# Moving w2's operand loads, the activation sums and their splits, and adding a fourth raw weight buffer, in a one-core transformer block

## The chip, the cores and the metric

One core of one Trainium2 chip runs the whole kernel in one launch. The metric is the device time of that core in microseconds: the median of several runs. One further execution was taken by the hardware profiler; its rows are quoted below. TensorE multiplies matrices, VectorE and ScalarE work element by element, GpSimd does so too and issues DMAs, SyncE issues DMAs.

## The reference

The input is 512 tokens of 2048 features. A mixing stage (differential attention beside a gated MLP) comes first and is not touched. What matters here follows it:

```
f = rms_norm(h, ffn_norm_g)
h = h + (silu(f @ ffn_w1) * (f @ ffn_w3)) @ ffn_w2     # 2048 -> 5632 -> 2048
h = h + (p @ pl_w_up) * sigmoid(h @ pl_w_gate)         # p has 256 features
return rms_norm(h, final_norm_g)
```

All values are float32.

## The kernel before

**Precision.** A float32 operand is written as a high part (a cast to float32r, made by ScalarE) and a low part (the rest, a subtraction on VectorE). `split` (lines 130 to 139) makes both. Each product is three matmuls: high x high, low x high, high x low. In the traces the weights' parts are called `whi` and `wlo`.

**Seven products.** The products with w1 and w3 together, w2 and w_gate are made by a scheme that computes a 2 x 2 block product with seven multiplications instead of eight. The weights' blocks come as four raw tiles of 512 KB each. Sums of blocks are made on VectorE as they are needed (`prepare`, lines 249 to 273, the subtractions in `sub`, line 240). The activations' sums are made once by `sums7` (lines 203 to 207): four additions or subtractions of 128 x 256 elements for each pair of feature tiles.

**The stream.** The function `stream` (lines 209 to 341) runs a list of phases as one sequence of steps: `up1` (2 plain steps for w_up), `up_proj` (w1 and w3, 11 groups), `down` (w2, 6 groups), `up2` (2 plain steps) and `gate` (2 groups). A group has 7 products i = 0 to 6 for each of its chunks of K; with 4 chunks that is 28 steps, with 3 chunks 21. `Phase` (lines 53 to 74) gives their order: i=0 leads and i=1 follows one chunk behind (steps 0 to 7), then i=2 and 3 (steps 8 to 15), 4 and 5 (16 to 23), and 6 (24 to 27). One step is 12 matmuls of 512 columns. In iteration `now` the code first prepares the weights of step `now + 2`, then emits the matmuls of step `now`, then the jobs that a table `at` or a call of `later` has put on this step. Tiles named `raw` hold a raw weight block (i=0, 2 and 5 load one; the one of i=2 is used again by i=3 of the same chunk); tiles with the tag `b12` hold the block loaded at i=0 until i=4. `whi` and `wlo` have three buffers each.

**The scheduler.** What is written is not the final order. Each instruction goes to its engine's queue in an order that a list scheduler makes at build time: among those whose operands are ready in its simulated time, the one written first is taken. On the chip each queue then runs strictly in order. `issue_after`, used by `behind`, holds an instruction behind another one. DMAs issued by `nc.sync` stand in SyncE's queue, those by `nc.gpsimd` in GpSimd's.

**Activations of the down projection.** After each group of `up_proj`, `swiglu` (lines 371 to 416) makes 512 features of silu(a) * b. `turn` transposes them on TensorE and copies them to a tile `t8`; `spread` (lines 391 to 399) makes the sums on GpSimd and four splits of at most two sums each, in a row, into tiles named `o7` (two buffers taken in turn: one in the pool `sp`, one with the tag `c21`), and stores each to the DRAM tensor `gs`. It runs 5 and 8 steps after the group's last step. The tag `c21` also holds the result of a group's last product.

**The down projection** takes its K in three parts of 4, 4 and 3 chunks (`kws`), and for each part two groups, one for each half of the columns; both use the same operand tiles `sop`. The job `load_s` (lines 939 to 943) brings them back from `gs` in the even group: `prepare_step` calls it, by `pre`, four steps (`LEAD`) ahead of the step prepared, so the text of the program has each pair of loads six steps before the step that uses it. `done2` adds each product to the residual `h`, which `load_h` brings from DRAM; `open_ev2` (step 12) closes the pool `sp` and loads four more tiles of `h` named `d`.

**Operands of gate.** In the last group of `down` (its first step is 133, `n5`) and in `up2`, finished parts of `h` are transposed by `turn_h`, summed by `sum_h` (on GpSimd for j = 0, 1, 2, 3, 6 and 4, on VectorE for 7 and 5) and split by `split_h` into the operand tiles. The transposes go to a tile `tg` (one buffer of its own) and one of `b12`, or to `c11` and `c21`.

**The start.** In `up1` the last squares for the norm are added up by GpSimd, `rms.token` sums them over the partitions with 8 small matmuls (line 441), and `late` makes the last operands. `swap` closes the pools of the stage before.

Of the kernel before, what the change touches and what calls it, by code (L numbers as in the profile page):

```python
# [19 lines left out]
P = 128  # L20
# [17 lines left out]
LEAD = 4  # L38
# [14 lines left out]
class Phase:  # L53
# [6 lines left out]
    def __init__(self, w=None, groups=(), op=None, done=None, late=False, pre=None, plain=None,  # L60
# [3 lines left out]
        self.pre, self.plain, self.at = pre, plain, at or {}  # L64
# [13 lines left out]
def block_kernel(ctx: ExitStack, tc: tile.TileContext, out, xT, pT, w_in, w_vg, w_out, w13, w2,  # L78
# [124 lines left out]
    def sums7(at, eng):  # L203

        for o, x, y, f in ((1, 7, 6, ALU.add), (4, 0, 7, ALU.subtract), (2, 1, 0, ALU.subtract),
                           (3, 5, 2, ALU.subtract)):
            eng.tensor_tensor(at(o), at(x), at(y), op=f)  # L207

    def stream(rp, hp, bp, tp, pp, phases, nraw=3, nhalf=3, kmax=KP // 2):
# [161 lines left out]
    def swiglu(ev, sp, r, gs):  # L371
# [511 lines left out]
    def evac_u(f0, tile):  # L883
        def evac(f, s, ps):
            o = tile(s)
# [22 lines left out]
    def jobs(*items):  # L908
        d = {}
        for n, fn, *a in items:  # L910
# [3 lines left out]
    up1 = Phase(plain=(pop, w_up[0:2], evac_u(0, lambda s: b7.tile(  # L914
        [P, 2, T], F32, name="up", tag="b12", bufs=KP // 2))), at=jobs(
            (0, last_squares), (0, late, sb, KP - EARLY, *kept[0]),
            (1, late, sb, KP - EARLY, *kept[1]), (1, lambda: r.append(rms.token())),
            (2, late, sb, KP - EARLY, *kept[2]), (3, swap)))
# [20 lines left out]
    def load_s(g, i, c):  # L939
        if g % 2 == 0:  # L940
            k = 2 * sum(kws[:g // 2]) + 2 * c
            for e in range(2):
                nc.gpsimd.dma_start(out=sop[2 * c + e][:, i], in_=gs[k + e, :, i])  # L943
# [33 lines left out]
    def sum_h(j, eng):  # L977
        sums7(lambda n: t7g[j][n // 4][:, n % 4], eng)
# [8 lines left out]
    n5 = 133  # L987
    dve, gps = nc.vector, nc.gpsimd
    down = Phase(w2, [(m, 2 * sum(kws[:n]), kw) for n, kw in enumerate(kws) for m in range(2)],
                 lambda g, k: seven(sop[k]), done2, pre=load_s, at=jobs(  # L990
                     (1, load_h, 0, 0), (6, load_h, 0, 1), (6, load_h, 1, 1), (10, load_h, 1, 0),
                     (12, open_ev2),
                     (n5 + 1, turn_h, 0, "tg"), (n5 + 2, sum_h, 0, gps),
                     (n5 + 3, split_h, 0, 0), (n5 + 3, split_h, 0, 1),
                     (n5 + 4, turn_h, 1, "tg"), (n5 + 5, sum_h, 1, gps),
                     (n5 + 6, split_h, 1, 0), (n5 + 6, split_h, 1, 1),
                     (n5 + 8, turn_h, 2, "tg"), (n5 + 9, sum_h, 2, gps),
                     (n5 + 10, turn_h, 3, "c"), (n5 + 11, sum_h, 3, gps),
                     (n5 + 13, split_h, 2, 0), (n5 + 14, split_h, 3, 0),
# [203 lines left out]
```

## Time and profile before

| what | value |
|---|---|
| median of 3 runs | 2217.76 us (2215.76 to 2220.18) |
| the profiled execution | 2219.64 us, of which 2217.9 from the first instruction to the last |
| TensorE busy with matmuls | 2147.3 us, 97% |
| VectorE busy | 1648.1 us, 74% |
| ScalarE busy | 1023.9 us, 46% |
| GpSimd busy | 387.4 us, 17% |
| mean granted TensorE clock | 0.992 of full speed |
| DMA traffic | 350.28 MB, 158 GB/s on the mean |

A busy share is a mean over stages of different kinds. Matmuls overlap in TensorE's pipeline, so a busy engine need not be at its peak. An idle engine is named with the engine or transfer that ended its wait.

The stages in the profiled execution start at: `up1` 680.4 us, `up_proj` 696.3 (its group 1 at 777.6, its group 10 at 1491.8), `down` 1577.7 (its group 1 at 1665.7, its group 5 at 1957.9), `up2` 2030.2, `gate` 2046.9; gate's last matmul starts at 2204.5.

### The profile page before, as it was taken

The page shows a single profiled execution, that of the slowest core. Times are in us where ns is not written, and L with a number is a line of the kernel's source. Part 1 is how long each engine was busy: PE and PEld are TensorE (multiplying, and loading weights), DVE is VectorE, ACT ScalarE, POOL GpSimd, SP SyncE. Part 2 cuts the span into 40 slices and gives each one's busy share as a digit, 9 for nine tenths or more (in the row PEclk, how much of TensorE's full clock was granted, in tenths as well). Part 3 has the DMA queues.
Part 4 walks back from the last instruction along what each step waited for, and adds up shares of the span by engine and source line. Part 5 has one row for each costly group of instructions (what it writes and reads, how often), then busy time and mean ns, then how long its engine had stood idle before and what let it go on. Part 6 is the DMA issues. An engine that isn't in the chain of part 4 may idle for free. (4 is left out here: it accounts for less than half of the span.)

```text
span 2217.9 us, 25518 instructions
## 1 busy us (share of the span) xinstructions
PE 2147.3 (97%) x9514; PEld 1749.2 (79%) x9514; DVE 1648.1 (74%) x1650; ACT 1023.9 (46%) x1295; POOL 387.4 (17%) x490
## 2 busy tenths in 40 slices
PE   7999999999999999999999999999999999998997
PEld 5788777878887888888888887887777788877785
DVE  8777664455436888878878878887877777787896
ACT  6354323445334455455455445544433333345555
POOL 4000300002221022022022112205403102033000
PEclk9999999999999999999999999999999999999999
DMA  5453532224445453553454444359758648435535
GB/s 171 152 159 98 189 95 76 83 69 129 138 137 185 115 172 123 161 179 131 138 187 142 127 168 162 128 173 305 252 195 259 206 138 265 142 109 188 182 106 181
DMA packets 112349, 350.28 MB, mean 158 GB/s; under 512 B 12976, under 2 KB 14512, under 8 KB 112224
## 3 DMA queue, kind: packets, MB, share of 16 engines
q1 hardware_dynamic: 67904, 233.86, 34.0%
q0 software_dynamic: 41056, 107.16, 14.3%
q10 hardware_dynamic: 3264, 7.62, 0.9%
q8 instruction: 75, 1.23, 0.2%
q14 instruction: 50, 0.41, 0.1%
HBM read 286.46 MB, written 62.13 MB: 157 GB/s over the span
## 5 line engine op out<-in xcount | busy, mean ns | idle before, releaser
L320 PE MATMUL c<-whi,op 128*128 128x512 f32 x4592 | 1427.5, 392 | 5.8 <-ACT whi L133 4.3
L320 PEld LDWEIGHTS c<-whi,op 128*128 128x128 f32 x4592 | 862.6, 189 | 184.2 <-ACT whi L133 5.1
L320 PE MATMUL c<-wlo,op 128*128 128x512 f32 x2296 | 903.2, 393 | 25.9 <-DVE wlo L134 25.2
L133 ACT CAST whi<-raw 128x1024 fp32r<-128x1024 f32 (+1 forms) x331 | 346.5, 1049 | 485.3 <-PE c L320 286.5
L134 DVE TENSOR_TENSOR wlo<-raw,whi 128x1024 fp32r<-128x1024 f32 (+1 forms) x331 | 417.2, 1265 | 199.4 <-ACT whi L133 194.5
L320 PEld LDWEIGHTS c<-wlo,op 128*128 128x128 f32 x2296 | 433.0, 189 | 134.9 <-DVE wlo L134 44.6
L133 ACT CAST whi<-t 128x1024 fp32r<-128x1024 f32 x246 | 258.6, 1052 | 271.4 <-PE c L320 244.3
L169 PE MATMUL ps<-op,whi 128*128 128x512 f32 x1088 | 349.0, 400 | 0.0
L134 DVE TENSOR_TENSOR wlo<-t,whi 128x1024 fp32r<-128x1024 f32 x246 | 308.3, 1255 | 22.0 <-ACT whi L133 21.5
L240 DVE TENSOR_TENSOR t<-raw,t 128x1024 f32<-128x1024 f32 x164 | 208.3, 1270 | 134.7 <-DMA raw<-w 115.4
L169 PEld LDWEIGHTS ps<-op,whi 128*128 128x128 f32 x1088 | 201.3, 188 | 44.3 <-issue 3.8
L169 PE MATMUL ps<-op,wlo 128*128 128x512 f32 x544 | 213.4, 392 | 0.0
L207 POOL TENSOR_TENSOR t<-t 128x256 f32<-128x256 f32 x88 | 106.5, 1210 | 541.1 <-ACT t L388 537.5
L133 ACT CAST whi<-b 128x1024 fp32r<-128x1024 f32 x82 | 86.3, 1054 | 123.3 <-PE c L320 114.7
L943 POOL DMA_DIRECT2D op<-gs x154 | 81.7, 535 | 298.5 <-PE c L320 284.3
L240 DVE TENSOR_TENSOR t<-b,raw 128x1024 f32<-128x1024 f32 x82 | 102.4, 1249 | 27.2 <-DMA raw<-w 23.4
L169 PEld LDWEIGHTS ps<-op,wlo 128*128 128x128 f32 x544 | 102.1, 188 | 21.6
L240 DVE TENSOR_TENSOR b<-raw,b 128x1024 f32<-128x1024 f32 x82 | 106.1, 1294 | 8.4 <-DMA raw<-w 7.5
L134 DVE TENSOR_TENSOR wlo<-b,whi 128x1024 fp32r<-128x1024 f32 x82 | 100.5, 1225 | 8.5 <-ACT whi L133 8.2
L133 ACT CAST o<-t 128x512 fp32r<-128x512 f32 x88 | 49.9, 567 | 105.6 <-DMA gs<-o 54.6
L344 DVE TENSOR_TENSOR c<-c,c 128x1024 f32<-128x1024 f32 x63 | 76.8, 1219 | 11.6 <-PE c L320 11.0
L453 POOL TENSOR_TENSOR r<-v,mhalf 128x1 f32<-128x1 f32 (+1 forms) x23 | 17.3, 752 | 383.7 <-DVE v L449 383.7
(177 smaller groups left out, 1321.2 us busy)
## 6 DMA issues: line engine op xcount, KB each, us to landing
raw<-w SPq DMA_DIRECT2D x198, 512.0 KB, 3.7
op<-gs POOLq DMA_DIRECT2D x154, 256.0 KB, 4.5
b<-w SPq DMA_DIRECT2D x66, 512.0 KB, 4.6
gs<-o POOLq DMA_DIRECT2D x66, 512.0 KB, 3.6
raw<-w_in SPq DMA_DIRECT2D x40, 512.0 KB, 3.6
raw<-w_out SPq DMA_DIRECT2D x32, 512.0 KB, 3.6
raw<-w_vg SPq DMA_DIRECT2D x24, 512.0 KB, 3.8
raw<-w_gate SPq DMA_DIRECT2D x24, 512.0 KB, 3.7
```

The source lines that it names most:

```text
L133: recent[:] = (nc.scalar.copy(out=hi, in_=src), nc.vector.tensor_tensor(out=lo, in0=src, in1=hi.bitcast(F32), op=ALU.subtract))
L134: nc.vector.tensor_tensor(out=lo, in0=src, in1=hi.bitcast(F32), op=ALU.subtract))
L169: nc.tensor.matmul(ps[:, m], lhsT=a[:, j, ms], rhs=op[k][:, b], start=k == 0 and i == 0, stop=k == nk - 1 and i == 2)
L207: eng.tensor_tensor(at(o), at(x), at(y), op=f)
L240: nc.vector.tensor_tensor(o, x, y, op=ALU.subtract)
L320: product[:] = [nc.tensor.matmul(p, lhsT=f.op(g, k)(i, x, s), rhs=y[:, e], start=k == 0 and i in (0, 1, 5) and (x, y) == (0, whi), stop=k ...
L344: (eng or nc.vector).tensor_tensor(o, x, y, op=ALU.add)
L453: nc.gpsimd.tensor_tensor(r[:, :n], v[:, :n], mhalf[:, :n], op=ALU.pow)
L943: nc.gpsimd.dma_start(out=sop[2 * c + e][:, i], in_=gs[k + e, :, i])
```

## The change

1. `stream` gets four raw buffers instead of three (`nraw=4`).
2. `load_s` is no longer called by `pre` six steps ahead. `loads` places each pair of loads in the table `at`: spread evenly from the first step of the group before the even group (a group of the part before, or the last of `up_proj`) to five steps ahead of the even group's end, though never ahead of the step after the old operand's last use.
3. `spread` is cut in parts: `add7` makes the sums, on VectorE, and each of the eight splits of a group has a step of its own, 5, 6, 8, 9, 11, 14, 17 and 20 steps after the group's end. Their `o7` tiles take the tags `c21` and `c12`; `sp` keeps only `t8`.
4. `sums7` always runs on VectorE, so `sum_h` goes into `split_h`; `both_h` makes both parts. Their places are moved by a step or so.
5. The tile `tg` is replaced by one of the raw buffers.
6. `load_h` and `open_ev2` are moved to later steps (1, 6, 10, 22 and 20).
7. In `up1`'s table `rms.token` moves from step 1 to step 4 and `swap` from 3 to 5, which are steps 2 and 3 of `up_proj`.
8. The evacuations of `up2` take `c12`, `c22`, a `b12` buffer and `c12`, instead of `c12` and `c22` twice.

```
-    def stream(rp, hp, bp, tp, pp, phases, nraw=3, nhalf=3, kmax=KP // 2):
+    def stream(rp, hp, bp, tp, pp, phases, nraw=4, nhalf=3, kmax=KP // 2):
...
-            if n + LEAD < len(steps) and steps[n + LEAD][0].pre:
-                f, *a = steps[n + LEAD]
-                f.pre(*a)
...
-        def spread(j, q):
+        def add7(q):
             t = c[q]
-            sums7(lambda n: t[:, n], nc.gpsimd)
-            for n in range(0, 7, 2):
-                m = min(2, 7 - n)
-                o = (ev[0].tile([P, 2, 2, 256], F32R, name="o7", tag="c21", bufs=1) if n % 4 else
-                     sp[0].tile([P, 2, 2, 256], F32R, name="o7", bufs=1))
-                split((o[:, :m, 0], o[:, :m, 1]), t[:, n:n + m])
-                nc.gpsimd.dma_start(out=gs[j, :, n:n + m], in_=o[:, :m].bitcast(F32))
+            sums7(lambda n: t[:, n])
+
+        def spread(j, q, n, tag):
+            m = min(2, 7 - n)
+            o = ev[0].tile([P, 2, 2, 256], F32R, name="o7", tag=tag, bufs=1)
+            split((o[:, :m, 0], o[:, :m, 1]), c[q][:, n:n + m])
+            nc.gpsimd.dma_start(out=gs[j, :, n:n + m], in_=o[:, :m].bitcast(F32))
...
-                    later(5 + 3 * q, spread, 2 * g + q, 2 * q)
+                    later(5 + 2 * q, add7, 2 * q)
+                    for k, n in enumerate((11, 14, 17, 20) if q else (5, 6, 8, 9)):
+                        later(n, spread, 2 * g + q, 2 * q, 2 * k, "c21" if q or k % 2 == 0 else "c12")
...
-            (1, late, sb, KP - EARLY, *kept[1]), (1, lambda: r.append(rms.token())),
-            (2, late, sb, KP - EARLY, *kept[2]), (3, swap)))
+            (1, late, sb, KP - EARLY, *kept[1]), (2, late, sb, KP - EARLY, *kept[2]),
+            (4, lambda: r.append(rms.token())), (5, swap)))
...
+    def loads():
+        for n, kw in enumerate(kws):
+            before = up_proj if n == 0 else down
+            last = [a[2:] for a in before.steps if a[1] == (2 * n - 1 if n else HT // 4 - 1)]
+            g0 = down.first[2 * n]
+            use = [a[2:] for a in down.steps if a[1] == 2 * n]
+            for j, (i, c) in enumerate(use):
+                t = -len(last) + j * (len(last) + len(use) - 6) // (len(use) - 1)
+                yield g0 + max(t, last.index((i, c)) - len(last) + 1), 2 * sum(kws[:n]) + 2 * c, 2 * c, i
...
-        if a == "tg":
-            t = (ev2[0].tile([P, 4, 256], F32, name="tg", bufs=1),
-                 b7.tile([P, 4, 256], F32, name="tg", tag="b12", bufs=KP // 2))
+        if a == "b":
+            t = [p.tile([P, 4, 256], F32, name="tg", tag=n, bufs=4) for p, n in ((w7, "raw"), (b7, "b12"))]
...
         if n:
             split((o[:, 4:7, 0], o[:, 4:7, 1]), t[:, 0:3])
         else:
+            sums7(lambda n: t7g[j][n // 4][:, n % 4])
             split((o[:, 0:4, 0], o[:, 0:4, 1]), t)
...
+    down.at.update(jobs((1, load_h, 0, 0), (6, load_h, 1, 1), (10, load_h, 0, 1),
+                        (20, open_ev2), (22, load_h, 1, 0),
+                        (n5 + 1, turn_h, 0, "b"), (n5 + 2, both_h, 0),
+                        (n5 + 4, turn_h, 1, "b"), (n5 + 5, both_h, 1),
+                        (n5 + 8, turn_h, 2, "b"), (n5 + 10, turn_h, 3, "c"),
+                        (n5 + 13, split_h, 2, 0), (n5 + 14, split_h, 3, 0),
...
+    def evac_tile(f, s):
+        p, n = (b7, "b12") if (f, s) == (1, 0) else (ev[0], "c22" if (f, s) == (0, 1) else "c12")
...
+        (0, split_h, 6, 1), (0, both_h, 7), (0, turn_h, 4, "b"),
+        (1, turn_h, 5, "c"), (1, both_h, 4)))
...
-                     (0, split_h, 5, 0), (0, split_h, 5, 1),
+                     (0, both_h, 5),
```

## Rows read from the trace of the kernel before

**Rows 1.** Windows: length, busy time and count per engine, clock, DMA share, GB/s.

```profile
core 0: us, PE busy (x) PEld busy (x) DVE busy (x) ACT busy (x) POOL busy (x), PEclk, DMA share, GB/s
680.40:777.60 97.20, 92.96 (x401) 75.74 (x401) 77.62 (x75) 47.63 (x51) 6.89 (x5) 0.96 0.47 146
777.60:1491.80 714.20, 708.64 (x3170) 579.93 (x3169) 587.83 (x531) 360.09 (x424) 127.08 (x144) 1.00 0.47 153
1491.80:1577.70 85.90, 80.86 (x353) 65.36 (x352) 65.75 (x59) 40.02 (x48) 42.43 (x72) 0.98 0.96 305
1577.70:1665.70 88.00, 82.20 (x353) 66.24 (x352) 67.02 (x60) 36.18 (x42) 18.22 (x25) 0.96 0.58 192
1665.70:1957.90 292.20, 288.00 (x1261) 235.91 (x1260) 224.81 (x193) 110.68 (x106) 53.36 (x101) 1.00 0.66 199
1957.90:2030.20 72.30, 66.06 (x301) 52.79 (x300) 60.91 (x49) 36.22 (x50) 30.86 (x24) 0.98 0.36 118
2030.20:2204.70 174.50, 167.86 (x737) 137.72 (x736) 149.11 (x142) 94.92 (x122) 6.26 (x8) 0.99 0.49 156
```

**Rows 2.** Windows of the streaming matmuls alone (line 320): PE, PEld, clock, DMA.

```profile
1755.00:1875.00 120.00, 120.00 (x531) 99.38 (x530) 1.00 0.57 171
2008.20:2011.20 3.00, 3.00 (x7) 2.42 (x8) 0.50 0.55 175
```

**Rows 3.** Timeline of TensorE: start, length, instruction, count.

```profile
703.97 1.03 PE L828 MATMUL pt<-ident,ho 128*128 128x128 f32 x8
```

**Rows 4.** Waits of TensorE, 680.4 to 2204.5: total, times, longest.

```profile
PE c L320 <- DVE wlo L134: 25.2, 28, 4.6
...
PE pt L968 <- ACT tg L975: 3.2, 1, 3.2
PE pt L441 <- POOL acc L432: 2.9, 1, 2.9
```

**Rows 5.** Waits of ScalarE, the same stretch.

```profile
ACT o L133 <- DMA gs<-o: 54.6, 30, 4.5
ACT o L133 <- POOL t L207: 51.0, 32, 2.7
```

**Rows 6.** Waits of VectorE, the same stretch.

```profile
DVE t L240 <- DMA raw<-w: 138.8, 80, 5.7
```

**Rows 7.** Timeline of VectorE in up group 7.

```profile
1297.54 1.22 DVE L240 TENSOR_TENSOR t<-raw,t 128x1024 f32<-128x1024 f32 x1 [2.51 <-DMA raw<-w]
1298.68 1.22 DVE L134 TENSOR_TENSOR wlo<-b,whi 128x1024 fp32r<-128x1024 f32 x1
1299.81 1.22 DVE L240 TENSOR_TENSOR t<-raw,t 128x1024 f32<-128x1024 f32 x1
```

**Rows 8.** Timeline of GpSimd, up group 10 and down group 0.

```profile
1531.92 6.05 POOL L943 DMA_DIRECT2D op<-gs  x11
...
1620.53 1.56 POOL L929 DMA_DIRECT2D d<-hnat  x3
```

**Rows 9.** All loads of line 943: durations, first and last start, landing times.

```profile
L943 POOL DMA_DIRECT2D op<-gs x154: 527/527/634, 1494.3 to 1897.6; - x154
...
DMA to landing us min/median/max: 2.9/4.5/9.6
```

**Rows 10.** Groups of VectorE by form, 696.3 to 2030.2: busy, mean ns, idle before.

```profile
L134 DVE TENSOR_TENSOR wlo<-raw,whi 128x1024 fp32r<-128x1024 f32 x198 | 252.6, 1282 | 59.6 <-ACT whi L133 59.3
L134 DVE TENSOR_TENSOR wlo<-t,whi 128x1024 fp32r<-128x1024 f32 x198 | 250.0, 1264 | 16.1 <-ACT whi L133 15.9
L240 DVE TENSOR_TENSOR t<-raw,t 128x1024 f32<-128x1024 f32 x132 | 169.2, 1282 | 115.9 <-DMA raw<-w 115.4
L240 DVE TENSOR_TENSOR b<-raw,b 128x1024 f32<-128x1024 f32 x66 | 86.7, 1313 | 8.4 <-DMA raw<-w 7.5
```

**Rows 11.** The sums of line 207: ns min/median/max, first and last start.

```profile
L207 POOL TENSOR_TENSOR t<-t x88: 724/1182/1830, 787.4 to 1606.3; 128x256 f32<-128x256 f32 x88
...
L207 DVE TENSOR_TENSOR c<-c x4: 407/410/411, 2031.7 to 2051.3; 128x256 f32<-128x256 f32 x4
```

More of the change, by code (lines that the diff above doesn't have):

```diff
@@ L53, with __init__ @@
 class Phase:
-    def __init__(self, w=None, groups=(), op=None, done=None, late=False, pre=None, plain=None,
+    def __init__(self, w=None, groups=(), op=None, done=None, late=False, plain=None,
                  at=None, order=None):
@@ L63, in __init__ @@
         self.w, self.groups, self.op, self.done, self.late = w, groups, op, done, late
-        self.pre, self.plain, self.at = pre, plain, at or {}
+        self.plain, self.at = plain, at or {}
         self.steps = [(self, -1, f, 0) for f in range(plain[1].shape[0])] if plain else []
@@ L201, in moving7, with sums7 @@
         return o
[L203 removed]
+    def sums7(at):
         for o, x, y, f in ((1, 7, 6, ALU.add), (4, 0, 7, ALU.subtract), (2, 1, 0, ALU.subtract),
                            (3, 5, 2, ALU.subtract)):
[L207 to L209 removed]
+            nc.vector.tensor_tensor(at(o), at(x), at(y), op=f)
+    def stream(rp, hp, bp, tp, pp, phases, nraw=4, nhalf=3, kmax=KP // 2):
         steps = [s for f in phases for s in f.steps]
@@ L884, in evac @@
         def evac(f, s, ps):
-            o = tile(s)
+            o = tile(f, s)
             with tc.high_priority(PRIO):
@@ L937, in open_ev2, with load_s @@
                 load_h(u, f)
[L939 to L943, printed above, removed]
+    def load_s(k, p, i):
+        for e in range(2):
+            nc.gpsimd.dma_start(out=sop[p + e][:, i], in_=gs[k + e, :, i])
+    def loads():
[7 more added lines that the diff above has]
+                yield g0 + max(t, last.index((i, c)) - len(last) + 1), 2 * sum(kws[:n]) + 2 * c, 2 * c, i
     def done2(g, i, acc, later, s=slice(None)):
@@ L984, in split_h, with both_h @@
         else:
+            sums7(lambda n: t7g[j][n // 4][:, n % 4])
             split((o[:, 0:4, 0], o[:, 0:4, 1]), t)
-    n5 = 133
-    dve, gps = nc.vector, nc.gpsimd
+    def both_h(j):
+        for n in range(2):
+            split_h(j, n)
     down = Phase(w2, [(m, 2 * sum(kws[:n]), kw) for n, kw in enumerate(kws) for m in range(2)],
[L990 to L999, printed above, removed]
-                     (n5 + 17, load_p),
-                     (n5 + 18, split_h, 2, 1), (n5 + 18, turn_h, 6, "tg"),
-                     (n5 + 19, split_h, 3, 1), (n5 + 19, sum_h, 6, gps), (n5 + 19, turn_h, 7, "c"),
-                     (n5 + 20, sum_h, 7, dve), (n5 + 20, split_h, 6, 0)))
@@ L1004, in block_kernel @@
-    up2 = Phase(plain=(pop, w_up[2:4], evac_u(2, lambda s: ev[0].tile(
-        [P, 2, T], F32, name=("c12", "c22")[s], bufs=1))), at=jobs(
-            (0, split_h, 6, 1), (0, split_h, 7, 0), (0, split_h, 7, 1),
-            (0, turn_h, 4, "tg"), (0, sum_h, 4, gps),
-            (1, turn_h, 5, "c"), (1, sum_h, 5, dve),
-            (1, split_h, 4, 0), (1, split_h, 4, 1)))
-    assert down.first[5] == n5
+                 lambda g, k: seven(sop[k]), done2)
+    n5 = down.first[5]
+    down.at.update(jobs((1, load_h, 0, 0), (6, load_h, 1, 1), (10, load_h, 0, 1),
[4 more added lines that the diff above has]
+                        (n5 + 13, split_h, 2, 0), (n5 + 14, split_h, 3, 0),
+                        (n5 + 17, load_p),
+                        (n5 + 18, split_h, 2, 1), (n5 + 18, turn_h, 6, "b"),
+                        (n5 + 19, split_h, 3, 1), (n5 + 19, turn_h, 7, "c"),
+                        (n5 + 20, split_h, 6, 0)))
@@ new lines, in block_kernel @@
+    for n, *a in loads():
+        f, n = (up_proj, n + len(up_proj.steps)) if n < 0 else (down, n)
+        f.at.setdefault(n, []).append((load_s, a))
+    def evac_tile(f, s):
+        p, n = (b7, "b12") if (f, s) == (1, 0) else (ev[0], "c22" if (f, s) == (0, 1) else "c12")
+        return p.tile([P, 2, T], F32, name="up", tag=n, bufs=4 if p is b7 else 1)
+    up2 = Phase(plain=(pop, w_up[2:4], evac_u(2, evac_tile)), at=jobs(
+        (0, split_h, 6, 1), (0, both_h, 7), (0, turn_h, 4, "b"),
+        (1, turn_h, 5, "c"), (1, both_h, 4)))
@@ L1017, in extra @@
     def extra(tag):
-        return {"b12": b7, "raw": w7, "tg": ev2[0], "d": ev2[0]}[tag].tile(
-            [P, 2, T], F32, name="last", tag=tag, bufs={"raw": 3, "tg": 1}.get(tag, 4))
+        return {"b12": b7, "raw": w7, "d": ev2[0]}[tag].tile([P, 2, T], F32, name="last", tag=tag, bufs=4)
     def load_last(u, f, *tags):
@@ L1118, in block_kernel @@
                      (43, load_last, 0, 3, "b12", "b12"), (46, load_last, 1, 3, "b12", "b12"),
-                     (47, load_last, 1, 2, "tg", "raw"), (49, load_gains, 2),
+                     (48, load_last, 1, 2, "raw", "raw"), (49, load_gains, 2),
                      (50, load_last, 0, 2, "raw", "raw")))
```

5 lines of the change are left out of this document (1 added, 4 removed).

## The prediction

> **What bounds the kernel now.** I read the stages first, then TensorE's waits, then what each waited-for engine was itself waiting for. The change touches nothing before 680.4 us except the size of one buffer ring, and nothing after TensorE's last gate matmul at 2204.7, so only this stretch counts. In a stretch without a wait, 529 matmuls start in 120 us (531 records touch the window, two of them only at its edges), 0.2267 us each [rows 2]; eight transposes take 1.03 us with the pipeline's tail of the last, about 0.11 each [rows 3]. A streaming step is 12 matmuls, 2.72 us. A stage's length less its matmuls and transposes at these prices is what TensorE lost there, slow clock included [rows 1]:
>
> - start (two plain steps, first up group): 97.2 - 384 x 0.2267 - 16 x 0.11 = 8.4
> - up groups 1 to 9: 714.2 - 3024 x 0.2267 - 144 x 0.11 = 12.8
> - up group 10: 85.9 - 336 x 0.2267 - 16 x 0.11 = 8.0
> - down group 0, the same work: 88.0 - 77.9 = 10.1
> - down groups 1 to 4: 292.2 - 1260 x 0.2267 = 6.6
> - down group 5: 72.3 - 252 x 0.2267 - 48 x 0.11 = 9.9
> - the two later plain steps and gate: 174.5 - 720 x 0.2267 - 16 x 0.11 = 9.5
>
> The sum, 65 us or 2.9%, is the ceiling of any gain here. The reader is to see that TensorE is the bound and that the losses are local. It waits mostly for `wlo`, VectorE's half of a weight split (25.2 us in 28 waits), once for an accumulator (2.9), once for a copy of `tg` (3.2) [rows 4]. A long wait costs twice: just after TensorE's waits around 2007, the granted clock is 0.50, the lower of its two levels (1.2 of 2.4 GHz), and seven matmuls fill 3 us [rows 2].
>
> Behind `wlo` stand two things. VectorE sits idle for a raw weight tile, 80 times, 138.8 us together, up to 5.7 [rows 6], while a released buffer refills; in [rows 7] it waits 2.51 us for one tile and only then makes the subtraction and the `wlo` that TensorE needs. And ScalarE, which casts `whi` in the same queue, stands still in the splits of the activations: 54.6 us for stores to `gs` out of the two `o7` buffers and 51.0 for GpSimd's sums [rows 5].
>
> **The fourth raw buffer.** Of a chunk's four loads three pass through `raw`: for steps i=0, 2 and 5. The i=2 tile lives until i=3. Within a group of 28 steps, with three buffers, the fourth i=2 load (used at step 13) gets the buffer freed at step 10; those for steps 18 and 20 get buffers freed at 12 and 14. With four, every chunk keeps its own buffer and the same loads are freed at 5, 10 and 12: at least 8 steps or 22 us ahead instead of 3 or 8.2 us. The slowest `op<-gs` transfer took 9.6 us to land [rows 9], and raw transfers share the same DMA engines. So I take these waits as nearly gone; bounds: none, if something else holds the queue of SP, and all.
>
> **The loads of w2's operands.** 154 DMAs before and after. Now the first leaves at 1494.3 [rows 9], just after step 0 of up group 10; its place in the program is near step 22 of that group (down step -6). So the emitted order runs such a load as soon as its slot's last reader is done, some 22 steps ahead of its place: two per step through one whole group. Group 10 thus moves 305 GB/s at a DMA share of 0.96, while the groups before it move 153 [rows 1]; when GpSimd's queue was held by `gs` stores, eleven loads left at once at 1531.92 [rows 8]. The new places lie at most 22 steps behind the same dependence. I therefore hold it more likely than not (6 in 10) that the loads still leave at once and the spreading does little. It matters only if raw loads are late, which the fourth buffer prevents; value 0, bounds 0 to the 11 us of the rival below.
>
> **Sums on VectorE.** 112 sums leave GpSimd (88 of swiglu at a median of 1.18 us, the others of the last down group and of the second plain phase). On VectorE one takes 0.41 [rows 11]: 112 x 0.41 = 46 us. Against it stands what GpSimd takes from VectorE. A full subtraction takes 1.22 us where GpSimd is idle [rows 7]; in this stretch the four groups average 1282, 1264, 1282 and 1313 ns [rows 10], an excess of 198 x 0.062 + 198 x 0.044 + 132 x 0.062 + 66 x 0.093 = 35 us, and the half-size splits add to it. So VectorE's total barely changes.
>
> The rows show a stretch of the overlapped instructions. The Trainium skill (SBUF — State Buffer, Who interferes with whom) goes further: a VectorE instruction with two SBUF inputs and a GpSimd one that reads SBUF contend for an exclusive port, and the loser blocks for the whole instruction. By that, as an estimate, VectorE could win back up to 112 x 1.18 = 132 us instead of 35, the waits left in up groups and down group 5 below would go too, and the sum would be near 2172, still inside the forecast's band; the measured averages do not show that much.
>
> What counts is the backlog at the worst place. Starts of full operations lie 1.14 us apart [rows 7]; half-size splits I put at 0.6. TensorE needs `wlo` 0.45 us into a step, and ScalarE may cast `whi` two steps earlier (three buffers), so VectorE's lead is 2 x 2.72 + 0.45 - 1.05 (cast) - 1.22 = 3.6 us. In steps 4 to 9 of a group the new order asks VectorE for 3.4, 1.7, 5.1, 4.0, 1.5 and 3.4 us (preparation of the step two ahead, 4 x 0.41 for `add7` in steps 4 and 6, splits) against 2.72 per step, 3.16 in steps 4 and 5 with their transposes. The backlog peaks at 3.6, just the lead: I leave half a microsecond per group, 5 us over groups 1 to 9. Splits every few steps also let each `gs` store land before its buffer is wanted, which takes the 54.6 us away from ScalarE's queue; the 51.0 shrink to VectorE's shorter sums.
>
> **Down group 5 and after.** The same count with `both_h` (4 x 0.41 + 1.14 + 0.88) in steps 2 and 5 peaks at 7.0, 3.4 over the lead; later splits and gate's first steps with `both_h` 4 and 5 exceed it by some 2.5. So 5 us of 9.9 stay, and 6 of 9.5 (the end of gate keeps its own). The evacuation that reused `c12`, behind the 3.2 us wait, goes to another buffer.
>
> **Start.** The accumulator's wait (2.9) and the half-clock step behind it (2.2) go when the token's matmuls come three steps later; TensorE then meets VectorE's work on the last operands earlier, so I count 4.3 of 8.4. **Down group 0.** Its loss follows a burst of `d` loads at 1620.53 [rows 8], which now leaves near step 20; with raw tiles held early I leave 2.5 of 10.1. Up group 10 keeps 1.5 of 8.0, down groups 1 to 4 keep 2 of 6.6. Moved loads of `h` change queue places, not counts; GpSimd's queue gets emptier. Should `c12` come back late for step 13, VectorE's addition would hold its queue; its cover is about 1.5 steps, and without it the cost is one such wait, some 4 us.
>
> **Sum.** 4.1 (start) + 5 + 1.5 + 2.5 + 2 + 5 + 6 = 26 us stay of 65: a gain of 39. The profiled execution took 2219.64 (span 2217.9), so 2180.4; the median of the runs, 2217.76, lies 1.9 lower, which gives 2178.5. I say 2180 because a new order of all queues seldom comes without one new wait.
>
> **Rivals.**
> - *The loads still come in a burst and starve the weights.* The demand in group 10 is some 336 GB/s, 26 MB in 78 us, near what [rows 1] show at a share of 0.96. Then group 10 and down 1 to 4 keep their losses: 2180 + 11 = 2191. Against it: 8 steps of lead. 0.11.
> - *The ring is not used*, since SP issues in order and a load of `b` waits at its head. Then up groups 1 to 10, down 1 to 4 and half of down group 0 keep theirs: 23 us of the gain go, 2203. 0.11.
> - *VectorE becomes the bound (slower).* It decides at the lead of 3.6 us: if the excess in [rows 10] is not GpSimd's doing, the sums come on top, 3.3 us per group; each up group waits that long and then runs a step at the lower clock (2.5): 11 x 5.8 = 64, down group 5 another 7, less 39: 2252. For it: the backlog count stands exactly at the lead. Against it: 1.22 without GpSimd in [rows 7]. 0.08. The Trainium skill (Perfetto Trace Analysis, Optimizing Scalar/DVE Operations) speaks for this rival: work may be offloaded from a saturated VectorE, to GpSimd even, though it adds that the shared port can spoil that; VectorE is busy 82% in [rows 1], and the change goes the other way.
> - *All waits vanish*: 2155. 0.07. *Gains and new waits cancel*: about 2217. 0.05.
> - The forecast, between 2167 and 2190: 0.58.
>
> **Range and chances.** 0.2% (4.4 us) is about what a measurement of this kernel can tell from no change. The range leaves out the slower rival, the cancelling one and most of the case where all waits vanish: 2160 to 2207. Faster: 0.58 + 0.11 + 0.11 + 0.07 = 0.87; same 0.05; slower 0.08.
>
> **What would show it.** Right: VectorE's waits for raw tiles fall from 138.8 to under 40 us; ScalarE's waits for `gs` stores are gone; full subtractions average 1.22; no accumulator wait ahead of up step 0. The loads' first start and the rate in up group 10 tell whether they spread. Wrong: waits for `wlo` in steps 6 to 10 of every group would mean that VectorE's backlog was undercounted; raw transfers landing after more than 15 us would mean that the DMA engines were.

## The result, and the profile after

2186.68 us median (2183.3 to 2187.53) against 2218.97 (2215.76 to 2221.66) for the kernel before on the same chip: a ratio of 0.9852, interval 0.9834 to 0.987. The profiled execution took 2185.85 us, its span 2183.7. The forecast was 2180, its range 2160 to 2207.

The stages of the kernel after, in windows (length, busy time and count per engine, clock, DMA share, GB/s), answer to [rows 1]:

```profile
core 0: us, PE busy (x) PEld busy (x) DVE busy (x) ACT busy (x) POOL busy (x), PEclk, DMA share, GB/s
684.10:785.90 101.80, 94.14 (x401) 75.77 (x402) 76.37 (x74) 46.25 (x51) 6.92 (x5) 0.95 0.41 129
785.90:1488.70 702.80, 702.80 (x3170) 581.63 (x3169) 581.81 (x603) 362.55 (x424) 38.70 (x72) 1.00 0.49 155
1488.70:1571.50 82.80, 78.83 (x354) 64.40 (x352) 64.56 (x67) 40.06 (x48) 34.09 (x64) 1.00 1.00 317
1571.50:1651.70 80.20, 79.14 (x354) 64.27 (x353) 66.52 (x68) 35.82 (x43) 8.90 (x17) 1.00 0.61 210
1651.70:1937.30 285.60, 285.60 (x1262) 236.49 (x1261) 225.57 (x192) 110.87 (x106) 54.55 (x101) 1.00 0.66 203
1937.30:2001.70 64.40, 63.47 (x302) 52.07 (x301) 60.02 (x68) 37.21 (x51) 2.13 (x4) 1.00 0.36 120
2001.70:2170.20 168.50, 166.18 (x737) 136.30 (x735) 148.79 (x147) 94.30 (x121) 2.25 (x3) 1.00 0.50 164
```

TensorE's loss in a stage is its length less matmuls at 0.2267 us and transposes at 0.11, as in the prediction. The same sum over windows of every later run gives this table; the first column is the start of the first plain matmul, "up", "down" and "gate" are the stages of [rows 1].

```
                      first  start up1-9  up10 down0 down1-4 down5 gate   sum
before                680.4    8.4  12.8   8.0  10.1     6.6   9.9  9.5  65.3
forecast                 -     4.1   5     1.5   2.5     2     5    6    26
after                 684.1   12.9   1.5   4.9   2.2     0.0   2.0  3.6  27
1  pT first           681.2    8.2   1.6   2.9   1.6     0.9   2.0  2.9  20
2  ring of three      680.5    7.4   5.3   9.6   1.1     8.3   2.2  4.0  38
3  old token          684.3   14.5   2.8   4.1   1.7     0.9   2.0  3.2  29
4  sums on GpSimd     683.5   14.0  11.1   7.4   6.4     1.0   2.0  3.0  45
5  after, again       683.7   14.3   1.5   5.9   2.8     1.0   2.0  3.0  31
7  splits bunched     677.9    8.0   6.6   3.6   7.1     0.3   2.0  2.1  30
8  splits early       679.2    9.1   5.8   7.7   6.1     1.0   2.0  2.8  35
9  loads held         679.2    8.2   1.5   7.3   4.9     0.2   2.0  3.4  28
10 tiles moved        679.6    9.3  14.2   6.3   1.6     6.1   2.9  5.6  46
11 squares on VectorE 679.3    7.9   1.5   4.0   0.9     0.5   2.0  3.0  20
12 no loads           678.9    9.1   2.4   0.2   0.2     2.1   2.0  2.4  18
```

(Runs 1, 7 to 12 hold pT first as well; run 6 stands with run 9.) Each row comes from one execution. Two executions of the same kernel, "after" and 5, differ by up to 1.4 us in a stage, so a difference of that size is read only where a wait in the trace accounts for it.

What the reader is to see: the gain that the forecast counted is there, and more, except in up group 10, which kept 4.9 us instead of 1.5, and at the start, which lost instead of gaining. Over the whole stretch TensorE's waits for `wlo` fall from 25.2 us to 7.1, and the one for `tg` is gone:

```profile
PE c L316 <- DVE wlo L133: 7.1, 7, 2.5
```

At the start, 684 to 786 us, TensorE's waits (total, times, longest) are these, to hold against [rows 4]:

```profile
PE c L316 <- ACT op L198: 5.7, 2, 4.9
PE c L298 <- ACT pop L132: 4.7, 1, 4.7
PE c L316 <- DVE op L199: 1.2, 1, 1.2
```

The accumulator's wait of 2.9 is gone. In its place TensorE waits 4.7 us for `pop`, the operand of the plain matmuls, made from the transfer of pT, and 4.9 and 1.2 at up step 6 for the last operand of the up half; behind each of them the granted clock is at or near its lower level, 0.58 from 684.1 to 687.5 and 0.51 from 722 to 729 (window, columns as above):

```profile
722.00:729.00 7.00, 4.18 (x9) 2.88 (x10) 6.26 (x5) 1.56 (x1) 0.00 (x0) 0.51 0.00 0
```

Why `pop` is late is on SyncE's queue. The kernel before, then after, in the timeline of its issues (start, length with its waits, transfer, count):

```profile
671.08 0.80 SPq L230 DMA_DIRECT2D raw<-w_up  x2
671.92 0.43 SPq L230 DMA_DIRECT2D raw<-w  x1
672.40 0.43 SPq L865 DMA_DIRECT2D pr<-pT  x1
```

```profile
669.95 0.80 SPq L229 DMA_DIRECT2D raw<-w_up  x2
670.80 6.63 SPq L229 DMA_DIRECT2D raw<-w  x4
677.48 0.43 SPq L863 DMA_DIRECT2D pr<-pT  x1
```

Before, the ring of three was full after three raw transfers, and pT came next. With a fourth buffer SyncE has four `raw<-w` to issue first, and waits among them for a buffer to come free; pT leaves 5.1 us later than before, lands 5.9 us after that, and the cast of `pop` starts at 683.4.

Waits of VectorE and of ScalarE, 684 to 2170, answer to [rows 6] and [rows 5]:

```profile
DVE t L239 <- DMA raw<-w: 64.7, 55, 3.1
DVE b L239 <- DMA raw<-w: 18.0, 20, 2.9
```

```profile
ACT o L132 <- DMA gs<-o: 48.1, 25, 5.8
ACT o L132 <- DVE t L206: 18.8, 11, 3.3
```

VectorE's groups by form, 700 to 2000 (busy, mean ns, idle before), answer to [rows 10], and the loads' first and last start and landing times to [rows 9]:

```profile
L133 DVE TENSOR_TENSOR wlo<-t,whi 128x1024 fp32r<-128x1024 f32 x197 | 240.2, 1220 | 27.8 <-ACT whi L132 26.2 <-PE pt L975 1.5
L133 DVE TENSOR_TENSOR wlo<-raw,whi 128x1024 fp32r<-128x1024 f32 x196 | 238.8, 1221 | 75.8 <-ACT whi L132 75.5
L239 DVE TENSOR_TENSOR t<-raw,t 128x1024 f32<-128x1024 f32 x132 | 161.3, 1222 | 65.3 <-DMA raw<-w 64.7
L239 DVE TENSOR_TENSOR b<-raw,b 128x1024 f32<-128x1024 f32 x66 | 80.6, 1221 | 18.5 <-DMA raw<-w 18.0
...
L133 DVE TENSOR_TENSOR o<-t,o 128x512 fp32r<-128x512 f32 x66 | 45.3, 686 | 5.9 <-ACT o L132 5.9
L206 DVE TENSOR_TENSOR t<-t 128x256 f32<-128x256 f32 x88 | 36.9, 419 | 0.0
```

```profile
L939 POOL DMA_DIRECT2D op<-gs x154: 540/540/554, 1491.2 to 1877.9; - x154
...
DMA to landing us min/median/max: 2.9/4.7/11.2
```

### The profile page after: what moved, and what is told of

It is laid out like the page before. It is cut to its first block, busy times and chain, and to the rows that moved or that the text cites. A ratio compares the mean times of both kernels' runs of the same rounds, so it can differ in the third digit from the quotient of the medians.

```text
span 2183.7 us, 25457 instructions
## 1 busy us (share of the span) xinstructions
PE 2130.8 (98%) x9514; PEld 1745.2 (80%) x9514; DVE 1640.0 (75%) x1762; ACT 1026.9 (47%) x1295; POOL 249.1 (11%) x378
## 5 line engine op out<-in xcount | busy, mean ns | idle before, releaser
L133 DVE TENSOR_TENSOR wlo<-raw,whi 128x1024 fp32r<-128x1024 f32 (+1 forms) x331 | 403.3, 1221 | 216.8 <-ACT whi L132 211.9
L316 PEld LDWEIGHTS c<-wlo,op 128*128 128x128 f32 x2296 | 431.3, 188 | 101.5 <-DVE wlo L133 11.2
L133 DVE TENSOR_TENSOR wlo<-t,whi 128x1024 fp32r<-128x1024 f32 x246 | 299.8, 1220 | 34.0 <-ACT whi L132 32.3
L239 DVE TENSOR_TENSOR t<-raw,t 128x1024 f32<-128x1024 f32 x164 | 200.5, 1222 | 78.4 <-DMA raw<-w 64.7
L395 POOL DMA_DIRECT2D gs<-o x88 | 47.3, 538 | 768.0 <-DVE o L133 718.1
L239 DVE TENSOR_TENSOR b<-raw,b 128x1024 f32<-128x1024 f32 x82 | 100.1, 1221 | 20.1 <-DMA raw<-w 18.0
L132 ACT CAST o<-t 128x512 fp32r<-128x512 f32 x88 | 49.1, 569 | 76.3 <-DMA gs<-o 48.1
L524 PE MATMUL c<-op,whi 128*128 128x512 f32 x192 | 61.9, 404 | 9.0 <-ACT whi L132 9.0
```

The source lines that it names most:

```text
L132: recent[:] = (nc.scalar.copy(out=hi, in_=src), nc.vector.tensor_tensor(out=lo, in0=src, in1=hi.bitcast(F32), op=ALU.subtract))
L133: nc.vector.tensor_tensor(out=lo, in0=src, in1=hi.bitcast(F32), op=ALU.subtract))
L239: nc.vector.tensor_tensor(o, x, y, op=ALU.subtract)
L316: product[:] = [nc.tensor.matmul(p, lhsT=f.op(g, k)(i, x, s), rhs=y[:, e], start=k == 0 and i in (0, 1, 5) and (x, y) == (0, whi), stop=k ...
L524: nc.tensor.matmul(ps[:, m], lhsT=a[:, n, m * P:(m + 1) * P], rhs=xop[k][:, b], start=k == 0 and i == 0, stop=k == KT - 1 and i == 2)
```

## The experiments

Ratios are to the kernel before in the same set of runs, whose median was 2213.18 us for runs 1 to 4, 2214.37 for 5 to 8, 2216.71 for 9 to 11 and 2215.51 for 12; beside the kernel after it was 2218.97, so times of different sets are compared by their ratios.

**1. pT first on SyncE's queue.**

```diff
-        nc.sync.dma_start(out=pr, in_=pT)
+        with tc.high_priority(10 * PRIO) if high else nullcontext():
+            nc.sync.dma_start(out=pr, in_=pT)
```

> The changed kernel, but the transfer of pT (1024 elements a row, the operand of the first plain matmuls) is put ahead of all raw transfers on SP's queue. Theory A (the fourth raw buffer let SP issue more raw transfers ahead of pT, and one of these waits for a slot, so pT is issued 5 us later than before and the start loses its gain): the first plain matmul moves back from 684.1 to about 680, the 4.7 us wait on the cast of pop goes, the half-clock step and the wait at up step 6 shrink with it; 2186.7 less about 8 is 2178 to 2180. Theory B (the moved rms token and swap, with the subtractions queued ahead of the last operand's sums on VectorE, make the start late): the first plain matmul comes earlier, but the wait at up step 6 grows by as much; 2185 to 2188.

2173.94 us, ratio 0.9823 (0.9807 to 0.9838), where the kernel after had 0.9852 and, in run 5, 0.9876. Timeline of SyncE's issues and TensorE's waits up to 777 us:

```profile
660.05 0.33 SPq L864 DMA_DIRECT2D pr<-pT  x1
671.89 0.80 SPq L229 DMA_DIRECT2D raw<-w_up  x2
```

```profile
PE c L316 <- DVE wlo L133: 2.9, 2, 1.8
PE c L316 <- ACT whi L132: 1.6, 1, 1.6
```

The waits for `pop` and at up step 6 are both gone: theory A. ScalarE's and VectorE's orders in this stretch shift a little with the new place, so whether step 6 was late only by the late plain steps or also by that order isn't separated. 4.5 us of other waits, at up steps 4 and 5, keep the start at a loss of 8.2.

This run also shows what the moved token is worth once pT is early. GpSimd's sum for the norm, then TensorE's first matmuls of up step 0:

```profile
693.34 4.63 POOL L430 TENSOR_TENSOR acc<-acc,sq 128x512 f32<-128x512 f32 x2 [26.43 <-ACT sq L429]
```

```profile
693.10 0.62 PE L316 MATMUL c<-whi,op 128*128 128x512 f32 x2
```

The sum ends at 697.97, 4.9 us after step 0 begins; in run 2, where pT is early too, it ends at 694.89 and step 0 begins at 691.86, 3.0 us. With the token ahead of step 0, as in the kernel before, TensorE would have had to wait some 3 to 5 us. This is an estimate from these rows: no run has tried the old token with pT early, and the old place could shift the sum as well.

**2. Three raw buffers** (small edits that fit the later users of the `raw` tiles to three buffers are left out here).

```diff
-    def stream(rp, hp, bp, tp, pp, phases, nraw=4, nhalf=3, kmax=KP // 2):
+    def stream(rp, hp, bp, tp, pp, phases, nraw=3, nhalf=3, kmax=KP // 2):
```

> The changed kernel with three raw buffers instead of four (the last load that had its fourth one gets a tile of its own). Theory A: the pT transfer is issued where it was before, so the start gets its 8 us back; but the waits for raw weights return everywhere else. The forecast priced the fourth buffer at 20 to 25 us, so 2186.7 - 8 + 23 = about 2200 (2193 to 2207), with VectorE's waits for raw weights back above 100 us. Rival (the sums that left GpSimd and the even stores took the stalls away, the fourth buffer did little): 2178 to 2184, VectorE's waits for raw weights near the changed kernel's 83 us.

2189.8 us, 0.989 (0.9873 to 0.9907). pT is issued at 672.14 and the first plain matmul starts at 680.5, without any priority: the second proof of what delayed it. Elsewhere the waits are back (VectorE, 681 to 2177):

```profile
DVE t L239 <- DMA raw<-w: 134.2, 92, 6.2
```

By the table, against run 1, up 1 to 10 and down 1 to 4 lose 23.2 instead of 5.4: the fourth buffer is worth 17.8 us. The time is 10 us under the 2200 expected: 5.8 is the chip, on which the kernel before was faster by that, and the forecast's 23 was some 5 too high. Of this 23, 3.8 stood for half of down group 0, which loses no more with three buffers (1.1) than with four (1.6).

**3. Token and swap at their old steps.**

```diff
-            (4, lambda: r.append(rms.token())), (5, swap)))
+            (1, lambda: r.append(rms.token())), (3, swap)))
```

> The changed kernel with the rms token and the swap of pools back at steps 1 and 3 of the first plain phase (from 4 and 5). Theory A (late pT): the start stays as late as it is, and the wait for the accumulator ahead of up step 0, some 4 us with its half-clock step, comes back: 2187 to 2191. Theory B (the moved token and swap cost the start): the wait at up step 6 of some 6 us goes, 2179 to 2183.

2187.55 us, 0.9888 (0.9871 to 0.9905). The waits at steps 5 and 6 stay (7.4 us for `op`, longest 4.8), the one for `pop` too, and 0.8 us for the accumulator come back. Theory B falls, and theory A is right on the late pT but not on its 4 us for the accumulator. Beside the late pT the plain steps end 5.0 us later than in the kernel before (696.8 for 691.7) and GpSimd's sum only 3.0 (697.55 for 694.55), so most of the wait is hidden: the 0.8 us is the price of the old place beside a late pT, and not beside an early one (run 1).

**4. The sums of the up half on GpSimd.**

```diff
-            sums7(lambda n: t[:, n])
+            sums7(lambda n: t[:, n], nc.gpsimd)
```

> The changed kernel with the activation sums of the up half (seven products' sums, 256 wide, four a tile) back on GpSimd; ring of four and spread splits stay. Theory A (the sums on GpSimd stretch VectorE's full operations and make the splits wait): full subtractions rise from 1.22 to about 1.28 us on average, the up groups lose 5 to 10 us again: 2190 to 2197. Rival (with the fourth buffer the stretch is covered, and VectorE is rid of 40 us of sums): 2184 to 2188.

2200.89 us, 0.9944 (0.9931 to 0.9958): slower than theory A asked for. Three groups of VectorE, 700 to 2000, its timeline beside GpSimd's sums in the eighth up group, the window of up groups 1 to 9, and ScalarE's waits:

```profile
L133 DVE TENSOR_TENSOR wlo<-t,whi 128x1024 fp32r<-128x1024 f32 x195 | 252.2, 1294 | 18.7 <-ACT whi L132 17.2 <-PE pt L975 1.5
...
L239 DVE TENSOR_TENSOR t<-raw,t 128x1024 f32<-128x1024 f32 x131 | 170.2, 1299 | 73.1 <-DMA raw<-w 71.5
...
L133 DVE TENSOR_TENSOR o<-t,o 128x512 fp32r<-128x512 f32 x66 | 56.1, 861 | 6.4 <-ACT o L132 6.3
```

```profile
1275.30 1.23 DVE L133 TENSOR_TENSOR o<-t,o 128x512 fp32r<-128x512 f32 x1
1276.45 1.75 DVE L239 TENSOR_TENSOR b<-raw,b 128x1024 f32<-128x1024 f32 x1
```

```profile
786.30:1498.80 712.50, 706.82 (x3170) 580.11 (x3169) 595.53 (x531) 361.66 (x424) 132.31 (x144) 1.00 0.47 153
```

```profile
ACT o L132 <- DMA gs<-o: 120.4, 57, 5.5
```

VectorE has 72 instructions fewer in up 1 to 9 and is busy 13.7 us longer: beside a sum, in these rows, a full operation takes 1.75 us instead of 1.22, and the half-size one that ends a split 1.23 instead of 0.69. ScalarE waits 120 us for the stores instead of 48; each store is released by such a split, but how much of the 72 us that explains wasn't taken apart. Up 1 to 10 and down 0 lose 24.9 instead of 10.2 in run 5.

**5. The kernel after once more**, without an edit.

> The changed kernel unchanged, on the chip of the three runs beside it, so that their ratios stand beside its own: 0.985 of the time before (0.983 to 0.987).

2187.62 us, 0.9876 (0.9857 to 0.9894): a little above the range expected, its interval overlapping that of the result (0.9834 to 0.987).

**6 and 9. Loads held to their steps.**

```diff
+        lo = ready[now + 1][1].bitcast(F32)[:, 0, 0:1]
+        v = sm.tile([P, 1], F32, name="held")
+        op = nc.gpsimd.tensor_tensor(v, lo, mhalf[:, 0:1], op=ALU.mult)
+        with tc.issue_after(op.ins):
             for e in range(2):
                 nc.gpsimd.dma_start(out=sop[p + e][:, i], in_=gs[k + e, :, i])
```

> The changed kernel with pT first (as in the first run) and with each pair of operand loads held to its planned step: a GpSimd operation of one column on the newest low half of the weights stands ahead of the two loads, so they can't leave before that step. Theory A (the loads leave two a step in the last up group because the queue has nothing to wait for; they slow the raw weights there): their first issue is spread over the group and the next, the raw weights land sooner, the last up group loses under 1.5 us instead of 2.9, the total is 1 to 3 us below the kernel with pT first alone (ratio 0.981 to 0.982). Theory B (the loads are hidden either way, and holding them only brings them nearer to their use): the last up group gains under 1 us and the down group after it loses as much or more; ratio 0.982 to 0.985.

2207.82 us, 0.9968 (0.9956 to 0.998), and the nine up groups, in which nothing is held, lost 14.2: an artefact, told with run 10. Run 9 writes `v` into a tile that was there:

```diff
-        v = sm.tile([P, 1], F32, name="held")
+        v = sm.tile([P, 4], F32, name="v")[:, 0:1]
```

> The held loads once more, with the GpSimd operation writing into a tile that was there already: in the run before, its own small tile moved every tile behind it by 128 bytes, and the matmuls of all up groups, nine of which have no held load in them, ran at a pitch of 230 to 240 ns instead of 227. Theory A (the moved tiles cost the pitch, the holding itself costs or gains little): the nine up groups are back at a loss under 3 us, the total is within 4 us of the kernel with pT first (ratio 0.980 to 0.984), and only now the loss of the last up group and of the first down group tells what an even return is worth (below 2.9 + 1.6 = 4.5 us: a gain). Theory B (the holding itself slows the whole, by its waits on the low halves): the time stays near the run before, ratio 0.994 to 0.998.

2180.83 us, 0.9842 (0.9829 to 0.9856), and up 1 to 9 are back at 1.5: theory A, as far as the place of the tiles goes. The windows of up 10 and down 0 show that the loads now do spread, 240 and 273 GB/s:

```profile
1479.10:1564.30 85.20, 80.83 (x353) 65.45 (x352) 64.41 (x67) 39.86 (x47) 39.14 (x57) 0.98 0.76 240
1564.30:1647.20 82.90, 79.66 (x354) 64.09 (x353) 66.70 (x68) 35.72 (x43) 29.34 (x51) 1.00 0.83 273
```

Yet both stages lose more, 7.3 and 4.9 us. GpSimd's timeline and then ScalarE's tell why:

```profile
1500.46 5.52 POOL L946 TENSOR_TENSOR v<-wlo,mhalf 128x1 f32<-128x1 f32 x1 [3.40 <-DVE wlo L133]
1505.92 1.11 POOL L949 DMA_DIRECT2D op<-gs  x2
1507.03 1.06 POOL L399 DMA_DIRECT2D gs<-o  x2
```

```profile
1513.01 0.41 ACT L132 CAST o<-t 128x256 fp32r<-128x256 f32 x1 [8.25 <-DMA gs<-o]
1513.32 1.04 ACT L132 CAST whi<-t 128x1024 fp32r<-128x1024 f32 x1
```

Two stores stand behind the holding operation, ScalarE waits 8.25 us for their buffer, and the cast that TensorE needs stands behind ScalarE's wait. So this hold costs, and the spreading itself was not yet priced; run 12 does that.

**7. The four splits of a tile at one step**, and **8. splits early**, both with two store buffers in turn:

```diff
-                    for k, n in enumerate((11, 14, 17, 20) if q else (5, 6, 8, 9)):
+                    for k, n in enumerate((8, 8, 8, 8) if q else (5, 5, 5, 5)):
```

(in run 8: 8, 9, 9, 10 and 5, 5, 6, 6)

> The changed kernel with pT first, and with the four splits of a tile at one step again (two buffers in turn), sums still on VectorE. Theory A (spreading is what keeps VectorE's backlog under its lead): sums and four splits in a row are 4 x 0.42 + 4 x 0.69, about 4.4 us of VectorE beside its regular work, twice a group; the nine up groups lose 5 to 15 us instead of 1.6, ratio 0.985 to 0.989. Rival (with the fourth raw buffer the lead covers it): groups lose 1 to 3 us as now, and ScalarE's waits for the stores, 48 us now, shrink, since two buffers take turns; ratio 0.981 to 0.983.

> The changed kernel with pT first, and the splits two at steps 5 and 6 and one to two at 8 to 10, two buffers in turn, so that all stores leave before the second half of a group. Theory A (ScalarE's waits for the one store buffer, at steps 11 to 20, hold up casts of the weights in the last up group, where loads make a store land in 6 us): ScalarE's waits for the stores fall below 25 us and the last up group loses about 1 us less than with pT first alone; the rest as there, ratio 0.981 to 0.982. Rival (a denser set of splits costs VectorE's lead): up groups lose 3 to 8 us instead of 1.6, ratio 0.983 to 0.986.

2186.46 us, 0.9874 (0.9858 to 0.989), and 2187.71, 0.9875 (0.986 to 0.989). Against run 1, up 1 to 9 lose 5.0 and 4.2 us more, and down 0 5.5 and 4.5. In run 8 up 10 also loses 4.8 more, which is not explained here. Most of the loss in down 0 is one wait of about 4 us, whose releaser the profile doesn't name. The rows ahead of it tell more; run 7's GpSimd, VectorE and TensorE:

```profile
1602.90 1.08 POOL L928 DMA_DIRECT2D d<-hnat  x2
```

```profile
1611.37 1.23 DVE L239 TENSOR_TENSOR t<-raw,t 128x1024 f32<-128x1024 f32 x1 [5.33 <-DMA raw<-w]
```

```profile
1614.97 0.70 PE L316 MATMUL c<-whi,op 128*128 128x512 f32 x2 [4.05 <-issue]
```

With the stores gone early, the loads named `d` leave 38.6 us into down 0 (53.8 in run 1), VectorE then waits 5.33 us for a raw tile, and TensorE's wait ends right behind. Run 8 has the same three: 37.8 us, 5.60 and 4.29. So the loss in down 0 looks like the old burst of `d` loads, come back because no store stands ahead of them in GpSimd's queue; no run moves these loads alone.

ScalarE's waits for the stores are 45.6 and 44.0 us where run 1 has 54.9, and its copies of an accumulator now wait for stores as well. Theory A of run 7 holds at its lower end in the up groups; in run 8 the rival does, a little slower yet than it said.

**10. All tiles moved by 128 bytes.**

```diff
+    nc.vector.memset(sm.tile([P, 1], F32, name="held"), 0.0)
```

> The kernel with pT first, and nothing else but a small tile of one column, cleared once at the start, which moves every tile allocated behind it by the same 128 bytes. Theory A (the place of the tiles sets the pitch): matmuls of the up groups at 230 ns and more on average, the nine up groups lose 10 to 15 us, ratio 0.99 to 0.996. Theory B (the place does not matter): as with pT first alone, 0.981 to 0.984.

2199.8 us, 0.9926 (0.9913 to 0.9938). Up groups 1 to 9 of run 1, then of this run:

```profile
778.20:1481.20 703.00, 703.00 (x3170) 581.62 (x3169) 581.77 (x603) 362.24 (x424) 38.62 (x72) 1.00 0.49 155
```

```profile
777.80:1493.30 715.50, 715.50 (x3169) 583.23 (x3168) 584.58 (x603) 362.42 (x424) 38.61 (x72) 1.00 0.48 152
```

TensorE is never idle in either, its clock is 1.00, and the same matmuls take 12.5 us longer. That is theory A, and it is what had spoilt run 6: less the transposes at 0.11 it is 0.2314 us a matmul instead of 0.2272. The streaming matmuls of no other run than 6 and 10 have the longer pitch, so the other comparisons are not touched by it. The profile shows no addresses; that the shift is 128 bytes is taken from the program.

**11. The last squares' additions on VectorE.**

```diff
-                nc.gpsimd.tensor_tensor(self.acc, self.acc, sq, op=ALU.add)
+                (eng or nc.gpsimd).tensor_tensor(self.acc, self.acc, sq, op=ALU.add)
```

> The kernel with pT first, and the two additions of squares in the first plain phase on VectorE (some 0.65 us each) instead of GpSimd (2.2 to 2.3 us each). Theory A (with pT first, what is left of the start's loss hangs on ScalarE's copy of the plain product, which waits 1.8 us for the tile that the second addition on GpSimd holds, and with it the casts, sums and the raw slots behind it): TensorE's waits at up steps 4 and 5, 4.4 us, and the half-clock stretch behind them shrink by 2 to 5 us; ratio 0.980 to 0.982. Rival (VectorE is the queue that is late there, and two more operations on it cost what they save): within 1 us of the kernel with pT first.

2176.42 us, 0.9819 (0.9806 to 0.9833): the same as run 1. The wait at step 4 goes, those at step 5 stay, and the start loses 7.9: the rival.

**12. Without the loads of the first chunk**, which this kernel leaves out.

```diff
     for n, *a in loads():
+        if n <= down.first[0] + 27:
+            continue
```

> The kernel with pT first, without the 56 operand loads of w2's first chunk (its products take what the up half left in those tiles), so that nothing returns in the last up group and the first down group; the loads of the two later chunks stay. It shows the most that any spreading of these loads can be worth. Theory A (the loads slow the raw weights and the stores there): TensorE's loss in the last up group falls from 2.9 to under 1 us and in the first down group from 1.6 to under 1 us, the total by 2 to 4 us; raw weights land in 3 to 4 us instead of 5 to 6.7. Theory B (what is lost there comes from the one store buffer and the waits on ScalarE): the loss stays within 1 us of the kernel with pT first alone, though transfers land sooner.

2170.92 us, 0.9797 (0.9783 to 0.981). Up 10 and down 0:

```profile
1480.50:1558.60 78.10, 78.10 (x353) 64.63 (x352) 64.57 (x67) 40.42 (x48) 4.83 (x9) 1.00 0.50 162
1558.60:1636.70 78.10, 78.10 (x353) 64.63 (x352) 66.72 (x68) 36.48 (x43) 8.02 (x15) 1.00 0.59 202
```

TensorE is busy throughout. Raw transfers land in 3.6 us (median) instead of run 1's 5.5. Theory A: the loads cost run 1 all but 0.4 us of its loss there, 4.1 us, and that is the most that spreading them can bring there. Leaving them out frees the DMA engines and GpSimd's queue, in which the stores stand, at once; which of the two counts for more isn't separated.

## Why the prediction was right, point by point

**The sum.** 26 us were to stay and 27 did, but TensorE's first plain matmul also came 3.7 us later, so the profiled execution is 5.5 us above the forecast 2180.4. That the sum came out so near is in part luck: the start and up 10 kept 12.2 us more than was counted, the other terms 11.2 less.

**Start: the term that was mis-sized.** It was to keep 4.1 of 8.4 us. It kept 12.9 and began 3.7 late, 12.5 us off. The reason given, that the accumulator's wait goes, was right, and its price of 2.9 us fits too: by the rows of runs 1 and 2 the move is worth some 3 to 5 us (an estimate) once pT is early, and 0.8 beside the late pT (run 3). What was overlooked is the fourth buffer's effect on SyncE's queue: the prediction asked which loads of the ring would come earlier, not which transfer outside the ring they would overtake. Runs 1 and 2 show it from both sides; pT first gives 2.9 + 4.7 = 7.6 us back by the profiles of this and of run 1. The rest is waits at up steps 4 and 5, where the run with pT first still loses; run 11 shows that GpSimd's additions are not the cause of those at step 5, and no run settles it.

**The fourth raw buffer.** Right in mechanism and in size in the up groups and down 1 to 4: 19 of the 23 us claimed were counted there, and run 2 shows 17.8. Wrong in down group 0, where half of the loss was put on the ring and run 2 shows none. "VectorE's waits for raw tiles under 40 us" was wrong: in the group of [rows 6] 64.7 us remain of 138.8, and with the waits of `b` 82.7 of 146.3; but they are covered, as up 1 to 9 and down 1 to 4 lose 1.5 us together. The rivals *ring not used* and *all waits vanish* are both out.

**Sums on VectorE.** Right: a full operation takes 1.22 us in all groups, and the excess in [rows 10] was GpSimd's doing, as run 4 brings it back. There the four groups of [rows 10] (means of 1294, 1248, 1299 and 1283 ns) exceed 1.22 by 195 x 0.074 + 195 x 0.028 + 131 x 0.079 + 66 x 0.063 = 34 us, and the half-size splits 0.686 by 66 x 0.175 = 12, together 46 us for 88 sums, 0.52 a sum, more than the 37 that these cost VectorE itself (88 of 0.419 in the kernel after).

The Trainium skill (SBUF — State Buffer, SBUF: two separate sides) has the loser of the shared port blocked for the whole instruction. By that, as an estimate, with run 4's mean of 1.286 us for a sum on GpSimd, it would be 88 x 1.286 = 113 us, where the trace shows 46. But that mean can hold waits of GpSimd's own: its sums took 0.735 to 1.821 us in run 4, and by the shortest it would be 65. The trace thus doesn't refute the block, and a delay of much the same length whatever the size of VectorE's operation looks more like one than like a slowing. The prediction's estimate of up to 132 us rests likewise on a median of 1.18, where [rows 11] has 0.724 as the shortest.

What the prediction didn't see is that ScalarE's waits for stores hang on the sums as well. The rival *VectorE becomes the bound* falls with up 1 to 9 at 1.5 us.

**Splits over steps.** The half microsecond left per group was 0.17. Run 7 prices the spreading at 5.0 us in up 1 to 9, where TensorE's waits are for `wlo` and, once, 1.4 us for a copy by ScalarE; the 5.5 us in down 0 seem to belong to the `d` loads. "ScalarE's waits for `gs` stores are gone" was wrong: 54.6 became 48.1. One buffer now carries most splits, but that this is why isn't shown: with two in turn, and denser splits, 45.6 and 44.0 stay (runs 7 and 8). They cost TensorE little where ScalarE has time, as up 1 to 9 show.

**The loads.** That they would still leave at once was right: the first starts at 1491.2, 2.5 us into up 10, and the stage moves 317 GB/s where [rows 1] had 305. That a ring of four makes this cost nothing was wrong by 3.4 us in up 10 (4.9 for 1.5): with the loads, raw tiles land in 5.7 us (median) and a store in 3.9 to 5, and ScalarE waits for the store with a weight's cast behind it. Run 12 shows the loads as the cause and 4.1 us as the stake: the rival *the loads still come in a burst* was right in kind, at a third of its 11 us. So "spread evenly" describes the program, not the execution.

**Down group 0.** 2.2 stayed where 2.5 were left. That its loss follows the burst of `d` loads fits runs 7 and 8, in which the burst and a wait of TensorE come back together. That the raw tiles held early help there isn't borne out (1.1 with three buffers, run 2), and the sums count too: with them on GpSimd it loses 6.4 (run 4).

**Down group 5, the plain steps and gate, down 1 to 4.** 2.0, 3.6 and 0.0 stayed where 5, 6 and 2 were left, so the count of VectorE's backlog was too cautious in the first two. The first two hold 13.8 of the 38 us gained, and no run takes apart which edits brought them (sums of gate's operands on VectorE, the new tiles for `tg` and the evacuations, the moved steps): here the cause is argued and not shown.

The version with pT first, 0.9823, beats both kernels; run 11 is level with it.

## What to carry to other kernels

One more buffer in a ring gives every transfer of that ring the right to be issued earlier, and on an in-order queue something else then waits: list what stands behind it, and put what TensorE needs first ahead of it. A place in the program holds a transfer back only if its queue has something to wait for; a hold built into a shared queue also holds what stands behind it. Work that goes from GpSimd to VectorE can make VectorE's total smaller, where the two ran side by side.

## What the runs showed of the hardware that was not expected

Beside GpSimd's sums most operations of VectorE took 0.42 to 0.55 us longer whatever their size, and the others no longer at all: 1.75 for 1.22, and 1.23 for 0.69 (run 4).

Moving all tiles behind one small one (by 128 bytes, as the program has it) made the same matmuls 1.8% slower with TensorE busy throughout at the full clock: 715.5 us against 703.0 for up 1 to 9 (3024 matmuls, 144 transposes), 291.8 against 286.6 for down 1 to 4, and 0.9926 against 0.9823 of the time before for the whole. Run 6 against run 9 shows it a second time (0.9968, 0.9842). Which pair of addresses matters wasn't tried. A kernel whose experiment adds a tile should be compared at the pitch of its matmuls first.
